# Scan and attention of a hybrid encoder block: one load a chunk, results gathered by the next stage's loads, output product first

## The chip, the cores and the metric

The kernel runs on one core of a Trainium2 chip. The time is device microseconds of one execution, the median of the runs. A core has TensorE (PE in the profile), VectorE (DVE), ScalarE (ACT), GpSimd (POOL) and SyncE (SP), which issues nearly all transfers of this kernel; 16 DMA engines carry them. Each engine works through a queue of its own in order, and so does SyncE: a transfer that waits for something holds up all that are queued behind it.

## What is computed

One layer for 2048 tokens of 1024 features and 16 learned meta tokens, float32. One input projection feeds two mixers side by side, their outputs are joined and projected, and a SwiGLU FFN follows:

```python
u = rmsnorm(h, g_mix[l]);  proj = u @ w_in[l]
na_q, na_k, na_v, dn_q, dn_k, dn_v, dn_z, dn_b, dn_a = jnp.split(proj, pts, axis=-1)
y_na = neighbourhood_attention(na_q, na_k, na_v, na_rel_bias[l], rows)   # 8 heads x 64, windows 8 x 16 of a 32 x 64 grid
y_dn = gated_deltanet(dn_q, dn_k, dn_v, dn_z, dn_b, dn_a, ...)           # 4 heads x 128, both directions, chunked scan
h = h + jnp.concatenate([y_na, y_dn], axis=-1) @ w_out[l]
u = rmsnorm(h, g_ffn[l])
h = h + (jax.nn.silu(u @ w_gate[l]) * (u @ w_up[l])) @ w_down[l]
return rmsnorm(h, g_final)[:, N_META:]
```

The scan goes over chunks of tokens with a state of 128x128 per head and direction. For each chunk:

```python
v_new = u_i - einsum('bhck,bhkv->bhcv', w_i, state)
o_i = einsum('bhck,bhkv->bhcv', q_i, state) + einsum('bhij,bhjv->bhiv', qk_i, v_new)
state = state * cd_i[..., None, None] + einsum('bhck,bhcv->bhkv', k_i, v_new)
```

The two directions are summed, normed and gated with z.

## The kernel before

It runs in three phases. **Phase A** (up to about 885 us) is the input projection, with the convolution, the gates and the chunks' triangular inverses beside it. It leaves its results in DRAM: for each of 16 chunks of 128 tokens and each head, `S.dx` holds four 128x128 blocks (raw queries transposed, keys transposed, keys, values), `S.qe` the queries with each direction's decay (`decays`, L846 to L865, stores them at L864), `S.xq` the inverse and the query-key product.

**Phase B** (885 to 1314 us) interleaves attention and scan by hand, in the loop of `phase_b` at L1325. Attention is 32 slots of 4 steps, a slot being one head and 512 queries. A step is scores (`att_s`, L1119 and L1120, then bias and row maximum on VectorE at L1123, the sign of the maximum on GpSimd at L1125, the exponential on ScalarE at L1126), transposition (`att_t`) and product with the values (`att_o`, L1147 to L1149). The score of a step runs two steps ahead of its product with the values. Query loads (`load_q`, L1055) have one buffer and are issued three steps ahead of `split`, which parts them into a high and a low half (ScalarE L1068, GpSimd L1069). Bias loads (`load`, L1062) have two buffers and leave at the first step of the slot before. Value loads (L1076) run four steps ahead. After every two slots the result tile `ys` goes to DRAM in `S.yo` (L1152), and `att_y` copies it from there, DRAM to DRAM, to its columns of `S.y` (L1165); the copy waits for the store to land.

The scan has 16 steps of 8 pieces (4 heads, 2 directions), one piece beside each attention step. `scan_load` (L1175) fetches the next step's two chunks, one for each direction, in three transfers each: keys and values (L1184, 768 KB), that direction's queries (L1186, 256 KB), and `xq` (L1187, 512 KB). The chunks of scan steps 4 to 7 stay in SBUF for steps 8 to 11, with the other direction's queries loaded into the same place. A piece is `scan_a` (keys times state, L1204, and a VectorE step, L1206), `scan_b` (L1214, then two copies to SBUF on ScalarE) and `scan_c`. The last puts two results in one PSUM tile: the state's update (L1236, read by VectorE at L1241) and then the output (L1244 with the old state, L1245), which ScalarE or VectorE takes out at L1249 or L1251. From scan step 8 on `norm` (L1263) norms two finished chunks and gates them with z (loaded at L1258, multiplied on GpSimd at L1259, then VectorE at L69 to L76 and L1284), and stores them to `S.y` (L1287). In scan steps 12 to 15 phase C's first part is called (`following`): it loads the eight pieces of `w_out` and parts them with ScalarE (L1394) and GpSimd (L1395, 128x1024 at a time), in buffers that the scan's chunks leave.

**Phase C** is the out-projection (1314 to 1517 us) and the FFN. For each of 16 row tiles, in the order 8 to 13, 0 to 7, 14, 15, `load` fetches 128 rows of `S.y` (L1433) and of x (L1435) two tiles ahead, `trans` transposes them (L1420, then L1422 and L1423), `project` multiplies with `w_out` (L1467), and `norm` and `finish` prepare the FFN's operands. The rest is the FFN (L1607 and L1683).

The order within each engine's queue is set by a scheduler from the program's order and its own estimates of times. Loads are tied behind the last value load (`A.last`) with `issue_after`.

Of the kernel before, what the change touches and what calls it, by code (L numbers as in the profile page):

```python
# [16 lines left out]
P = 128  # L17
# [804 lines left out]
def pre_unit(tc, S, Q, hp, half):  # L822
# [23 lines left out]
    def decays(n, kq, rows):  # L846
        a, g = divmod(n, 4)
        h, cg = 2 * hp + a, c0 + g * 2
        E = []
        for e, d in ((0, 0), (1, 1), (2, 1)):  # L850
            ex = Q.g.tile([P, 2, P], F32, name=f"E{e}")
            for c in range(2):
                nc.vector.tensor_scalar(ex[:, c], rows[d][:, c], S.gc[:, d * 4 + h, cg + c:cg + c + 1], 0.0,
                                        op0=ALU.subtract, op1=ALU.max if e == 1 else ALU.min)
            nc.scalar.activation(ex, ex, AF.Exp, scale=-1.0 if e == 1 else 1.0)
            if e != 1:
                s = 1 if e == 0 else -1
                nc.gpsimd.affine_select(out=ex, in_=ex, pattern=[[0, 2], [s, P]], compare_op=ALU.is_ge, fill=0.0,
                                        base=0, channel_multiplier=-s)
            E.append(ex)  # L860
        for d in range(2):
            nc.scalar.activation(rows[d], rows[d], AF.Exp)
            nc.gpsimd.tensor_tensor(rows[d], rows[d], kq[:, :, 0], ALU.mult)
            nc.sync.dma_start(S.qe[d, cg:cg + 2, h].rearrange("c p i -> p c i"), rows[d])  # L864
        return E  # L865
# [161 lines left out]
def attention_loads(tc, S, es, rel):  # L1027
# [36 lines left out]
    def split(n):  # L1064
        s = A.slots[n]
        s.q1 = kp.tile([P, 512], F32R, name="q1")
        s.q2 = kp.tile([P, 512], F32R, name="q2")
        nc.scalar.copy(s.q1, s.qr)  # L1068
        nc.gpsimd.tensor_tensor(s.q2, s.qr, s.q1, ALU.subtract)  # L1069
# [17 lines left out]
def phase_b(tc, S, A, W, norm_g, following):  # L1087
# [4 lines left out]
    with ExitStack() as es:  # L1092
# [46 lines left out]
        def att_o(i):  # L1139
# [10 lines left out]
            if a == 1 and k == 3:  # L1150
                n = i // 8
                nc.sync.dma_start(S.yo[n].rearrange("k r c e -> (r c) k e"), ys[0].rearrange("p k a d -> p k (a d)"))  # L1152
                yq.append((s, S.yo[n]))

        yq = []

        def att_y():

            while yq:
                s, yo = yq.pop()  # L1160
                e0 = s.h // 2 * P
                k = 0
                for C, R0, R1 in s.segs:
                    dst = S.y.rearrange("(g f c) d -> f g c d", f=4, c=16)[C, R0 * 8:R1 * 8, :, e0:e0 + P]
                    nc.sync.dma_start(dst, yo[k:k + R1 - R0].rearrange("k r c e -> (k r) c e"))  # L1165
                    k += R1 - R0
# [7 lines left out]

        def scan_load(s):  # L1175
            cs = (s, 15 - s)
# [5 lines left out]
            for d, c in enumerate(cs):  # L1182
                if c in new:
                    nc.sync.dma_start(dxt[c][:, :, 1:4], S.dx[c, :, :, 1:4].rearrange("h p a i -> p h a i"))  # L1184
                if s != 8:
                    nc.sync.dma_start(dxt[c][:, :, 0], S.qe[d, c].rearrange("h p i -> p h i"))  # L1186
                nc.sync.dma_start(xqt[d, c], S.xq[d, c].rearrange("h p a i -> p h a i"))  # L1187
# [6 lines left out]
        def scan_a(i):  # L1194
            s, h, d, c = geo(i)
            ld = dxt[c][:, h]
# [3 lines left out]
            if S_ is None:  # L1200
                sc[i] = ld[:, 3]
                return
            pa = pz_.tile([P, P], F32, name="z")
            nc.tensor.matmul(pa, ld[:, 1], S_, start=True, stop=True)  # L1204
            R = sp.tile([P, P], F32, name="R", bufs=3)
            nc.vector.scalar_tensor_tensor(R, pa, S.neg_eg[:, dh, col], ld[:, 3], op0=ALU.mult, op1=ALU.add)  # L1206
# [20 lines left out]
        def scan_c(i):  # L1227
# [6 lines left out]
            pc = pz_.tile([P, 2, P], F32, name="z")  # L1234
            if s < 15:
                nc.tensor.matmul(pc[:, 1], dxt[c][:, h, 2], vn[:, 1], start=True, stop=True)  # L1236
# [6 lines left out]
            if S_ is not None:  # L1243
                nc.tensor.matmul(pc[:, 0], dxt[c][:, h, 0], S_, start=True, stop=False)  # L1244
            done[i] = nc.tensor.matmul(pc[:, 0], xqt[d, c][:, h, 1], vn[:, 0], start=S_ is None, stop=True)  # L1245
            if s == 7:
                nc.sync.dma_start(dxt[c][:, h, 0], S.qe[1 - d, c, h])
# [5 lines left out]
        def norm_load(s):  # L1253
            N = Ctx()
            N.z = []
            for c in (s, 15 - s):
                z = sp.tile([P, 4, P], F32, name="z", bufs=2)
                nc.sync.dma_start(z, S.zx[c * P:(c + 1) * P, :].rearrange("p (h d) -> p h d", h=4))  # L1258
                nc.gpsimd.tensor_tensor(z, z, bc(S.ng.rearrange("p (o d) -> p o d", o=1), [P, 4, P]), ALU.mult)  # L1259
# [3 lines left out]
        def norm(s):  # L1263
# [17 lines left out]
            for j, c in enumerate(cs):  # L1281
# [5 lines left out]
                nc.sync.dma_start(S.y[c * P:(c + 1) * P, 512:1024].rearrange("p (h d) -> p h d", h=4), z)  # L1287
# [37 lines left out]
        for i in range(N + 4):  # L1325
# [6 lines left out]
            if i % 4 == 0 and i < 124:  # L1332
                with tc.issue_after(A.last.ins):
                    A.load(i // 4 + 1)
# [10 lines left out]
            if i % 4 == 3:  # L1345
                att_y()
# [28 lines left out]
def phase_c(tc, S, W, wes, x, w_out, g_ffn, w_gate, w_up, w_down, g_final, out):  # L1375
# [11 lines left out]
    with ExitStack() as ps_es:  # L1387
# [3 lines left out]
        def split(hl, src, eng=nc.vector):  # L1391
            raw = st.tile(list(src.shape), F32, name="yu")
            nc.sync.dma_start(raw, src)
            nc.scalar.copy(hl[:, 0], raw)  # L1394
            eng.tensor_tensor(hl[:, 1], raw, hl[:, 0], ALU.subtract)  # L1395
# [3 lines left out]
        for k in range(KB):  # L1399
            wo.append(split(W.tile([P, 2, D], F32R, name="w"), w_out[:, k], nc.gpsimd))  # L1400
# [29 lines left out]
        def load(j):  # L1430
            rows = slice(order[j] * P, (order[j] + 1) * P)
            yt = st.tile([P, D], F32, name="yu")
            nc.sync.dma_start(yt, S.y[rows, :])  # L1433
# [322 lines left out]
def scratch(tc, es):  # L1756
# [7 lines left out]
    S.yo = [dp.tile([4, 8, 16, P], F32, name=f"yo{i}") for i in range(16)]  # L1764
    S.zx = dp.tile([NT, 512], F32, name="zx")
    S.dx = dp.tile([16, 4, P, 4, P], F32, name="dx")
    S.qe = dp.tile([2, 16, 4, P, P], F32, name="qe")
# [4 lines left out]
    S.y = dp.tile([NT, D], F32, name="y")  # L1772
# [132 lines left out]
```

## Time and profile before

| | us |
|---|---|
| median of 3 runs | 2909.57 (2900.05 to 2914.04) |
| the profiled execution | 2900.0 |
| its span, first to last instruction | 2898.0 |
| TensorE busy | 2750.9 (95%) |
| VectorE busy | 1772.8 (61%) |
| ScalarE busy | 1170.8 (40%) |
| GpSimd busy | 754.4 (26%) |

All times below are from the start of the span. In a line of the order of time the engine comes before the source line, and what stands in brackets is how long the engine had been idle and what ended it. "x2" after a group's name means that two instructions were merged into one line, whose time then covers both. The granted clock is a share of TensorE's full 2.4 GHz; its other level is 1.2 GHz, so a mean between 0.5 and 1 tells how long it stood at either.

### The profile page before, as it was taken

The numbers are of one execution on the slowest core, as the hardware profiler recorded it, in microseconds if no ns is written. First come the engines' busy times: TensorE is split into PE (matmuls) and PEld (weight loads), VectorE is DVE, ScalarE is ACT, GpSimd is POOL, SyncE is SP. The second block draws the span as 40 slices with busy tenths as digits, with TensorE's granted clock in tenths as the row PEclk, the third lists the DMA queues.
The fourth block names the chain that finished last, engine by engine and source line by source line (L and its number), as shares of the span: only waits on it lengthen the run. The fifth ranks groups of instructions, "written<-read, shape, count | busy, mean of one in ns | idle before, by whom it ended". The sixth has DMA issues, their size and how long they took to land.

```text
span 2898.0 us, 45796 instructions
## 1 busy us (share of the span) xinstructions
PE 2750.9 (95%) x16364; PEld 2407.7 (83%) x16364; DVE 1772.8 (61%) x3900; ACT 1170.8 (40%) x2733; POOL 754.4 (26%) x769
## 2 busy tenths in 40 slices
PE   8999988988988989879999999999999999999998
PEld 8998988988888988868887888887887888888886
DVE  5897466895643546774667655554547665554354
ACT  4652333652415656752334333333434333233342
POOL 2353353341511112241225223210104322320010
PEclk9999999999999998979999999999999999999999
DMA  4675655566869988985535222236353222225452
GB/s 151 190 203 146 163 156 141 163 179 175 210 159 280 287 231 241 302 258 185 182 126 169 88 80 80 84 116 251 129 183 113 84 88 87 73 95 200 141 177 71
DMA packets 396096, 466.31 MB, mean 161 GB/s; under 512 B 92083, under 2 KB 300300, under 8 KB 394302
## 3 DMA queue, kind: packets, MB, share of 16 engines
q1 hardware_dynamic: 394142, 457.11, 52.0%
q0 software_dynamic: 1728, 6.29, 0.6%
q8 instruction: 129, 2.11, 0.3%
q14 instruction: 97, 0.79, 0.1%
HBM read 334.14 MB, written 141.15 MB: 164 GB/s over the span
## 4 chain that ended last, share of the span: by engine, by line
PE 53%; DVE 3%; DMA 2%; issue 1%; ACT 1%; POOL 0%; SPq 0%; DVEq 0%; ACTq 0%; POOLq 0%
PE pg L1607 24%; PE pg L1683 8%; PE pd L1467 6%; PE pd L1683 4%; PE tp L1683 4%; PE pd L1607 4%; PE y L1147 1%; DVE z L1284 1%; PE tp L1420 0%; DVE w L1451 0%; PE tp L1493 0%; DMA b<-in_rel_dram 0%; DMA k<-kx 0%; POOL s L1555 0%; PE y L1133 0%
## 5 line engine op out<-in xcount | busy, mean ns | idle before, releaser
L405 PE MATMUL acc<-uh,wf 128*128 128x384 f32 (+5 forms) x1920 | 470.0, 329 | 3.0 <-ACT uh L342 1.9
L1451 DVE TENSOR_TENSOR w<-rw,w 128x512 fp32r<-128x512 f32 x308 | 244.0, 794 | 251.2 <-ACT w L1450 250.4
L1607 PE MATMUL pg<-T,w 128*128 128x512 f32 x1584 | 393.9, 397 | 2.6 <-ACT T L1450 1.3
L1607 PE MATMUL pg<-B,w 128*128 128x512 f32 x1584 | 387.9, 397 | 3.5 <-ACT B L1450 2.9
L1450 ACT CAST w<-rw 128x512 fp32r<-128x512 f32 x308 | 190.3, 620 | 485.8 <-PE tp L1683 252.4
L1607 PEld LDWEIGHTS pg<-B,w 128*128 128x128 f32 x1584 | 299.0, 189 | 77.7 <-ACT B L1450 3.3
L1607 PEld LDWEIGHTS pg<-T,w 128*128 128x128 f32 x1584 | 298.2, 188 | 76.0 <-ACT T L1450 1.8
L405 PEld LDWEIGHTS acc<-uh,wf 128*128 128x128 f32 x1920 | 340.2, 192 | 5.7 <-ACT uh L342 2.0
L405 PE MATMUL acc<-ul,wf 128*128 128x384 f32 (+5 forms) x960 | 312.5, 326 | 0.0
L1683 PE MATMUL pg<-w,hT 128*128 128x512 f32 x1056 | 260.9, 395 | 1.9 <-ACT hT L1450 1.8
L1555 POOL TENSOR_TENSOR s<-rw 128x512 f32<-128x512 f32 x88 | 119.5, 1358 | 546.7 <-DMA rw<-in_w_gate_dram 262.4
L1683 PEld LDWEIGHTS pg<-w,hT 128*128 128x128 f32 x1056 | 198.1, 188 | 50.8 <-ACT hT L1450 2.2
L429 PE MATMUL acc<-wn,uh 128*128 128x256 f32 (+3 forms) x1056 | 209.9, 298 | 10.6 <-DVE vs L473 10.3
L1451 DVE TENSOR_TENSOR w<-s,w 128x512 fp32r<-128x512 f32 x176 | 131.6, 750 | 133.9 <-ACT w L1450 132.8
L1450 ACT CAST w<-s 128x512 fp32r<-128x512 f32 x176 | 108.6, 620 | 234.4 <-PE pg L1607 140.4
L405 PEld LDWEIGHTS acc<-ul,wf 128*128 128x128 f32 x960 | 184.8, 192 | 0.8
L429 PEld LDWEIGHTS acc<-wn,uh 128*128 128x128 f32 (+1 forms) x1056 | 172.6, 197 | 13.8 <-DVE vs L473 10.7
L499 DVE SCALAR_TENSOR_TENSOR ct<-cr,cw,ct 128x1024 f32<-128x1024 f32 (+1 forms) x96 | 138.0, 1444 | 37.4 <-ACT ct L497 36.3
L242 POOL TENSOR_TENSOR wf<-raw,wf 128x512 fp32r<-128x512 f32 x80 | 119.6, 1509 | 157.7 <-ACT wf L241 134.5
L1467 PE MATMUL pd<-w,yh 128*128 128x512 f32 x512 | 159.9, 394 | 0.0
L429 PE MATMUL acc<-wn,ul 128*128 128x256 f32 (+3 forms) x528 | 157.4, 298 | 2.4 <-DVE rx_i L58 2.4
L1621 DVE TENSOR_TENSOR eg<-pg,eg 128x512 f32<-128x512 f32 x110 | 76.0, 690 | 106.1 <-PE pg L1607 106.1
(359 smaller groups left out, 5325.8 us busy)
## 6 DMA issues: line engine op xcount, KB each, us to landing
rw<-in_w_down_dram SPq DMA_DIRECT2D x88, 512.0 KB
rw<-in_w_gate_dram SPq DMA_DIRECT2D x44, 512.0 KB
rw<-in_w_up_dram SPq DMA_DIRECT2D x44, 512.0 KB
hd<-eg SPq DMA_DIRECT2D x88, 256.0 KB
s<-hd SPq DMA_DIRECT2D x88, 256.0 KB
raw<-in_w_feat_dram SPq DMA_DIRECT2D x80, 256.0 KB
w<-dx SPq DMA_DIRECT2D x24, 768.0 KB
xq<-xq SPq DMA_DIRECT2D x32, 512.0 KB
```

What stands on the lines that cost most here:

```text
L242: nc.gpsimd.tensor_tensor(lo, raw, hi, ALU.subtract)
L405: nc.tensor.matmul(ps[:, 0:c1 - c0], hl[:, a, k, :], (U.h, U.l)[l][ci][:, k, c0:c1], start=(i == 0), stop=(i == 23))
L429: nc.tensor.matmul(ps[0:np_, 0:n], (U.h, U.l)[l][ci][:, k, off:off + np_], hl[:, a, k, 0:n], start=(i == 0), stop=(i == 23))
L499: nc.vector.scalar_tensor_tensor(tt, raw[:, j:j + T], cw[:, b, j:j + 1], tt, op0=ALU.mult, op1=ALU.add)
L1147: nc.tensor.matmul(po, t.pT[0:w, c], t.v[0:w, c], start=(c == 0), stop=(c == nch - 1))
L1450: nc.scalar.copy(dst_h, src)
L1451: eng.tensor_tensor(dst_l, src, dst_h, ALU.subtract)
L1467: nc.tensor.matmul(ps, (yh, yl)[a][:, k], wo[k][:, b, cs], start=(i == 0), stop=(i == 23))
L1555: nc.gpsimd.tensor_tensor(s, p, q, op)
L1607: nc.tensor.matmul(ps, w[:, a, k], t[:, b, k], start=(k == 0 and (a, b) == (0, 0)), stop=(k == 3 and a == 1))
L1621: nc.vector.tensor_tensor(dst, ps, x0, ALU.add)
L1683: nc.tensor.matmul(acc[j][hf], hk[f][:, a, j * P:(j + 1) * P], wk[f][hf][:, b], start=(f == 0 and i == 0), stop=(f == NFF - 1 and i == 2))
```

## The change

- `S.dx` gets a fifth block a chunk and head. The decayed queries of the forward direction replace the raw ones in block 0, those of the backward direction go to block 4, and `S.qe` is gone. A chunk's first load takes blocks 0 to 3 or 1 to 4 in one transfer of 1 MB; `place` says where queries, keys and values then lie. Only the other direction's queries are still loaded alone.
- In `scan_c` the output's two products come first, then the state's update.
- `S.yo` holds all attention results in one array by head pair, column block and row block. `att_y` is gone, and so are the attention's columns of `S.y`. The out-projection's `load` takes the scan's half of a tile with one transfer and the attention's half with eight, each of 16 partitions and 4 x 512 bytes.
- The bias load of slot n leaves at the last step of slot n - 2 instead of the first step of slot n - 1.
- The subtractions on GpSimd at L1069 and L1259 are done in two halves each. Those at L1395 go to VectorE and, with ScalarE's copies at L1394, are done in halves of 128x512.

```diff
@@ decays
-            nc.sync.dma_start(S.qe[d, cg:cg + 2, h].rearrange("c p i -> p c i"), rows[d])
+            nc.sync.dma_start(S.dx[cg:cg + 2, h, :, 4 * d].rearrange("c p i -> p c i"), rows[d])
@@ split (queries)
-        nc.gpsimd.tensor_tensor(s.q2, s.qr, s.q1, ALU.subtract)
+        for c in (slice(0, 256), slice(256, 512)):
+            nc.gpsimd.tensor_tensor(s.q2[:, c], s.qr[:, c], s.q1[:, c], ALU.subtract)
@@ att_o, att_y
             if a == 1 and k == 3:
-                n = i // 8
-                nc.sync.dma_start(S.yo[n].rearrange("k r c e -> (r c) k e"), ys[0].rearrange("p k a d -> p k (a d)"))
-                yq.append((s, S.yo[n]))
...
-            while yq:
-                s, yo = yq.pop()
-                e0 = s.h // 2 * P
                 k = 0
                 for C, R0, R1 in s.segs:
-                    dst = S.y.rearrange("(g f c) d -> f g c d", f=4, c=16)[C, R0 * 8:R1 * 8, :, e0:e0 + P]
-                    nc.sync.dma_start(dst, yo[k:k + R1 - R0].rearrange("k r c e -> (k r) c e"))
+                    nc.sync.dma_start(S.yo[s.h // 2, C, R0:R1].rearrange("k r c e -> (r c) k e"),
+                                      ys[0][:, k:k + R1 - R0].rearrange("p k a d -> p k (a d)"))
                     k += R1 - R0
@@ scan_load
                 if c in new:
-                    nc.sync.dma_start(dxt[c][:, :, 1:4], S.dx[c, :, :, 1:4].rearrange("h p a i -> p h a i"))
-                if s != 8:
-                    nc.sync.dma_start(dxt[c][:, :, 0], S.qe[d, c].rearrange("h p i -> p h i"))
+                    place[c] = (0, 1, 2, 3) if d == 0 else (3, 0, 1, 2)
+                    nc.sync.dma_start(dxt[c], S.dx[c, :, :, d:d + 4].rearrange("h p a i -> p h a i"))
+                elif s != 8:
+                    nc.sync.dma_start(dxt[c][:, :, place[c][0]], S.dx[c, :, :, 4 * d].rearrange("h p i -> p h i"))
@@ scan_c
+            q, k = (dxt[c][:, h, place[c][n]] for n in (0, 2))
+            if S_ is not None:
+                nc.tensor.matmul(pc[:, 0], q, S_, start=True, stop=False)
+            done[i] = nc.tensor.matmul(pc[:, 0], xqt[d, c][:, h, 1], vn[:, 0], start=S_ is None, stop=True)
             if s < 15:
-                nc.tensor.matmul(pc[:, 1], dxt[c][:, h, 2], vn[:, 1], start=True, stop=True)
+                nc.tensor.matmul(pc[:, 1], k, vn[:, 1], start=True, stop=True)
...
-            if S_ is not None:
-                nc.tensor.matmul(pc[:, 0], dxt[c][:, h, 0], S_, start=True, stop=False)
-            done[i] = nc.tensor.matmul(pc[:, 0], xqt[d, c][:, h, 1], vn[:, 0], start=S_ is None, stop=True)
             if s == 7:
-                nc.sync.dma_start(dxt[c][:, h, 0], S.qe[1 - d, c, h])
+                nc.sync.dma_start(q, S.dx[c, h, :, 4 * (1 - d)])
@@ norm_load, norm
-                nc.gpsimd.tensor_tensor(z, z, bc(S.ng.rearrange("p (o d) -> p o d", o=1), [P, 4, P]), ALU.mult)
+                for h in range(0, 4, 2):
+                    nc.gpsimd.tensor_tensor(z[:, h:h + 2], z[:, h:h + 2], bc(S.ng.rearrange("p (o d) -> p o d", o=1), [P, 2, P]), ALU.mult)
...
-                nc.sync.dma_start(S.y[c * P:(c + 1) * P, 512:1024].rearrange("p (h d) -> p h d", h=4), z)
+                nc.sync.dma_start(S.y[c * P:(c + 1) * P, :].rearrange("p (h d) -> p h d", h=4), z)
@@ the loop of phase_b
-            if i % 4 == 0 and i < 124:
+            if (i == 0 or i % 4 == 3) and i < 120:
                 with tc.issue_after(A.last.ins):
-                    A.load(i // 4 + 1)
+                    A.load((i + 1) // 4 + 1)
...
-            if i % 4 == 3:
-                att_y()
@@ phase_c
-        def split(hl, src, eng=nc.vector):
+        def split(hl, src):
             raw = st.tile(list(src.shape), F32, name="yu")
             nc.sync.dma_start(raw, src)
-            nc.scalar.copy(hl[:, 0], raw)
-            eng.tensor_tensor(hl[:, 1], raw, hl[:, 0], ALU.subtract)
+            for c in (slice(0, 512), slice(512, D)):
+                nc.scalar.copy(hl[:, 0, c], raw[:, c])
+                nc.vector.tensor_tensor(hl[:, 1, c], raw[:, c], hl[:, 0, c], ALU.subtract)
...
-            wo.append(split(W.tile([P, 2, D], F32R, name="w"), w_out[:, k], nc.gpsimd))
+            wo.append(split(W.tile([P, 2, D], F32R, name="w"), w_out[:, k]))
@@ load (out-projection)
-            nc.sync.dma_start(yt, S.y[rows, :])
+            nc.sync.dma_start(yt[:, 512:], S.y[rows, :])
+            for r in range(2):
+                for C in range(4):
+                    p = r * 64 + C * 16
+                    R, rr = divmod(order[j] * 2 + r, 8)
+                    nc.sync.dma_start(yt[p:p + 16, 0:512].rearrange("c (h e) -> c h e", h=4),
+                                      S.yo[:, C, R, rr].rearrange("h c e -> c h e"))
@@ scratch
-    S.yo = [dp.tile([4, 8, 16, P], F32, name=f"yo{i}") for i in range(16)]
-    S.dx = dp.tile([16, 4, P, 4, P], F32, name="dx")
-    S.qe = dp.tile([2, 16, 4, P, P], F32, name="qe")
+    S.dx = dp.tile([16, 4, P, 5, P], F32, name="dx")
-    S.y = dp.tile([NT, D], F32, name="y")
+    S.y = dp.tile([NT, 512], F32, name="y")
+    S.yo = dp.tile([4, 4, 4, 8, 16, P], F32, name="yo")
```

## Rows read from the trace of the kernel before

**Rows 1.** Stretches of the span: busy us (instructions) of PE, PEld, DVE, ACT, POOL; clock, DMA share, GB/s

```profile
885.00:1228.00 343.00, 307.29 (x2365) 296.97 (x2366) 199.77 (x805) 219.57 (x718) 68.31 (x141) 0.94 0.93 271
...
1228.00:1314.00 86.00, 66.87 (x440) 62.83 (x439) 65.55 (x214) 49.87 (x146) 35.12 (x41) 0.80 0.83 265
...
1314.00:1517.00 203.00, 203.00 (x1014) 168.62 (x1012) 117.28 (x247) 59.10 (x109) 38.48 (x29) 1.00 0.48 156
```

**Rows 2.** Order of time on TensorE, its longest gaps, 885 to 1270

```profile
982.99 0.49 PE L1214 MATMUL z<-R,xq 128*128 128x128 f32 x2 [4.46 <-ACT oacc L1249]
...
1021.22 0.80 PE L1244 MATMUL z<-S,w 128*128 128x128 f32 x2 [3.25 <-DVE S L1241]
...
1087.80 0.80 PE L1204 MATMUL z<-S,w 128*128 128x128 f32 x2 [3.89 <-ACT oacc L1249]
...
1197.11 0.79 PE L1244 MATMUL z<-S,w 128*128 128x128 f32 x2 [4.41 <-DVE S L1241]
...
1238.91 0.79 PE L1204 MATMUL z<-S,w 128*128 128x128 f32 x2 [6.38 <-DVE R L1206]
...
1266.09 0.79 PE L1244 MATMUL z<-S,w 128*128 128x128 f32 x2 [4.83 <-DVE R L1206]
```

**Rows 3.** Order of time on ScalarE and VectorE, where two of these gaps begin

```profile
981.24 0.62 ACT L1068 CAST q<-qr 128x512 fp32r<-128x512 f32 x1 [5.00 <-DMA qr<-qx]
...
1020.34 0.56 DVE L1123 CUSTOM_DVE_ANT_0 sb<-y,b 128x384 f32<-128x384 f32 x1 [5.00 <-DMA b<-in_rel_dram]
```

**Rows 4.** Order of time on GpSimd and VectorE, 1259 to 1282

```profile
1259.87 4.66 POOL L1395 TENSOR_TENSOR w<-yu,w 128x1024 fp32r<-128x1024 f32 x2 [6.01 <-PE z L1204]
...
1260.19 2.08 DVE L75 TENSOR_SCALAR or_t<-or_t 128x8 f32<-128x8 f32 x1
...
1275.01 1.13 DVE L1284 SCALAR_TENSOR_TENSOR z<-oacc,of,z 128x128 f32<-128x128 f32 x4
...
1276.13 5.36 DVE L1284 SCALAR_TENSOR_TENSOR z<-oacc,of,z 128x128 f32<-128x128 f32 x4
```

**Rows 5.** Waits from 880 to 1320 (SyncE 1330): who for whom, us total, times, longest

```profile
SPq L1165 <- DMA yo<-ys: 24.8, 11, 4.1
...
DVE sb L1123 <- DMA b<-in_rel_dram: 17.0, 7, 5.0
...
PE z L1244 <- DVE S L1241: 11.9, 8, 4.4
```

**Rows 6.** Order of time of SyncE's issues

```profile
963.97 0.38 SPq L1152 DMA_DIRECT2D yo<-ys  x1
...
969.45 0.56 SPq L1165 DMA_DIRECT2D y<-yo  x1
...
972.42 1.09 SPq L1055 DMA_DIRECT2D qr<-qx  x2
...
1195.61 1.69 SPq L1055 DMA_DIRECT2D qr<-qx  x2
```

**Rows 7.** Transfers from 885 to 1314: queue (packets, MB, share), issues (KB each)

```profile
q1 hardware_dynamic: 97607, 115.27, 90.7%
...
y<-yo SPq DMA_DIRECT2D x12, 256.0 KB
...
y<-yo SPq DMA_DIRECT2D x6, 128.0 KB
```

**Rows 8.** Line L1451: count, ns min/median/max, first and last start

```profile
L1451 DVE TENSOR_TENSOR w<-s,w x176: 676/692/1777, 1519.6 to 2619.9; 128x512 fp32r<-128x512 f32 x176
```

**Rows 9.** Order of time, out-projection: a tile's load on SyncE, its transposition on TensorE

```profile
1345.33 0.33 SPq L1433 DMA_DIRECT2D yu<-y  x1
...
1356.31 0.60 PE L1420 MATMUL tp<-ident,yu 128*128 128x128 f32 x4
...
1360.16 0.58 SPq L1433 DMA_DIRECT2D yu<-y  x1
...
1369.02 0.60 PE L1420 MATMUL tp<-ident,yu 128*128 128x128 f32 x4
```

More of the change, by code (lines that the diff above doesn't have):

```diff
@@ L1150, in att_o @@
             if a == 1 and k == 3:
-                n = i // 8
-                nc.sync.dma_start(S.yo[n].rearrange("k r c e -> (r c) k e"), ys[0].rearrange("p k a d -> p k (a d)"))
-                yq.append((s, S.yo[n]))
-        yq = []
-        def att_y():
-            while yq:
-                s, yo = yq.pop()
-                e0 = s.h // 2 * P
                 k = 0
                 for C, R0, R1 in s.segs:
-                    dst = S.y.rearrange("(g f c) d -> f g c d", f=4, c=16)[C, R0 * 8:R1 * 8, :, e0:e0 + P]
-                    nc.sync.dma_start(dst, yo[k:k + R1 - R0].rearrange("k r c e -> (k r) c e"))
+                    nc.sync.dma_start(S.yo[s.h // 2, C, R0:R1].rearrange("k r c e -> (r c) k e"),
+                                      ys[0][:, k:k + R1 - R0].rearrange("p k a d -> p k (a d)"))
                     k += R1 - R0
@@ L1173, in phase_b @@
         dxt, xqt, sc = {}, {}, {}
+        place = {}
         def scan_load(s):
@@ L1195, in scan_a @@
             s, h, d, c = geo(i)
-            ld = dxt[c][:, h]
+            kT, v = (dxt[c][:, h, place[c][n]] for n in (1, 3))
             col = slice(c, c + 1)
@@ L1200, in scan_a @@
             if S_ is None:
-                sc[i] = ld[:, 3]
+                sc[i] = v
                 return
             pa = pz_.tile([P, P], F32, name="z")
-            nc.tensor.matmul(pa, ld[:, 1], S_, start=True, stop=True)
+            nc.tensor.matmul(pa, kT, S_, start=True, stop=True)
             R = sp.tile([P, P], F32, name="R", bufs=3)
-            nc.vector.scalar_tensor_tensor(R, pa, S.neg_eg[:, dh, col], ld[:, 3], op0=ALU.mult, op1=ALU.add)
+            nc.vector.scalar_tensor_tensor(R, pa, S.neg_eg[:, dh, col], v, op0=ALU.mult, op1=ALU.add)
             sc[i] = R
```

## The prediction

> **What bounds the kernel now.** I read the page's slices first (TensorE is nearly full everywhere, least so around the attention and scan), then the busy time by stretch. Three stretches matter [rows 1]: attention beside scan (885 to 1228 us), the scan's end with its norms and the attention that is left (1228 to 1314), and the out-projection (1314 to 1517). In the third TensorE is busy for all 203.0 us at a granted clock of 1.00: nothing can be won there, only lost. In the first it is idle for 343 - 307.3 = 35.7 us, and its clock of 0.94 stretches the busy part by about 307.3 x 0.06 = 18 us. In the second it is idle for 86 - 66.9 = 19.1 us, and the clock of 0.80 costs about 66.9 x 0.2 = 13 us. So 86 of the 2898 us can be touched at all. The transfers are no free resource: the DMA share is 0.93 in the first stretch and 0.83 in the second.
>
> The order of time on TensorE says where the idle time lies [rows 2]. In the first stretch four gaps of 3.25 to 4.46 us make 16.0 of the 35.7 us. TensorE waits for ScalarE or VectorE there, but those had been waiting themselves [rows 3]: ScalarE 5.00 us for a query load at 981.24, VectorE 5.00 us for the bias at 1020.34; the other two gaps look the same. These are late loads. In the second stretch the two longest gaps, 6.38 and 4.83 us, end on VectorE, which was not waiting but slow: at 1260.19 an operation on 128x8 elements took 2.08 us while GpSimd ran two subtractions of L1395 in 4.66 us, and at 1276.13 four multiplies of L1284 took 5.36 us where the four before took 1.13 [rows 4].
>
> **The change, part by part.** All sums are against the profiled execution: a span of 2898.0 in a run of 2900.0 us. The median of the runs shown is 2909.57, 9.6 above it.
>
> *Results gathered by the out-projection.* The 20 copies from yo to y go, and with them their waits: SyncE stood 24.8 us for L1165, 11 times [rows 5]. Behind it in its queue stand the bias, the queries and the values. In front of the gap at 983 a store to yo is issued at 963.97, the copy leaves at 969.45, the queries at 972.42 [rows 6] and land at 981.2: without the wait (24.8/11 = 2.3 us) and the copy's 0.56 us they leave nearly 3 us sooner. In DMA time the queue was busy for 90.7% of 429 us = 389 us [rows 7]; the copies that fall in it are 12 x 256 + 6 x 128 KB = 3.9 of its 115.27 MB, or 7680 of its 97607 packets of 512 B. That is 13 us by bytes and 31 by packets; I take the byte end, the smaller gain.
>
> *One load a chunk.* By the code 24 of the 30 query loads of the scan (256 KB in pieces of 512 bytes, so 512 packets) join their chunk's load: 12288 packets fewer and no byte. Its worth lies between 0 and 12288/97607 x 389 = 49 us of DMA time; I take 0 by the same choice. A first load of 1 MB instead of 768 KB delays the scan's first matmul by about 1 us (256 KB at the 271 GB/s of [rows 1]). The stores to the strided slot in the input projection are as many and as long; TensorE doesn't wait for them, so 0, at most a few us if their landing held the next loads.
>
> *Bias one step earlier.* 32 bias loads leave one step of 429/128 = 3.35 us sooner. The waits of 5.00 us shrink to about 1.7. The new place can wait for VectorE to have read the buffer's last user, on SyncE, with value and key loads behind it; the value loads wait there for a TensorE step of the same age anyhow, so I cost it at nothing, at most a step (3.35 us) where they don't cover it.
> For the four gaps together I take 10 of 16.0 us: 6 of the 7.7 us that end on the bias, 4 of the 8.3 us on queries. A us of idle time brought 18/35.7 = 0.5 us of slow clock in this stretch: 5 us more.
>
> *Output first.* TensorE waited 11.9 us at L1244 for VectorE's state update, 8 times [rows 5]: the two products share a PSUM tile, and the second was started after the first had been read. Two of the eight are gaps on the bias counted above (3.25 and 4.41), so 4.2 us are left; I take 3. The state comes later by two products, but is wanted eight scan steps on: 0.
>
> *Subtractions from GpSimd to VectorE, and in halves.* Eight subtractions of w_out go from GpSimd; six lie in the second stretch. VectorE gets 16 of 128x512, 0.69 us each by the same form in the FFN [rows 8]: 11 us, 12 of them (8.3 us) in the second stretch, where VectorE has 65.6 busy in 86 us, a good part of it the stretched operations. The remaining GpSimd operations in halves hold VectorE up for about half as long. I take 60% of the 19.1 us idle, 11 us, with 13/19.1 = 0.7 us of clock for each, 8 us; and half of the 8.3 us of new VectorE work on the path, -4. The bounds are 0 (new work takes the place of what it held up) and 32 (all idle and slow time).
> The Trainium skill, page "SBUF — State Buffer", section "Who interferes with whom", has a rule for this: a VectorE instruction with two SBUF inputs and a GpSimd instruction that reads SBUF exclude each other, and whoever is first keeps the other out for a whole instruction. The rows agree. By it the new subtraction, with two SBUF inputs, is itself held up by what stays on GpSimd, which speaks for the -4.
>
> *The out-projection's loads.* Each of 16 row tiles now takes 9 loads for y instead of one: 128 more issues. Two issues together took 1.09 us [rows 6], so a tile's nine take about 5 us. A landing took 969.45 - 963.97 - 0.38 = 5.1 us in the full queue: an upper bound, since the DMA share is 0.48 here [rows 1]. The time at hand is 11.0 us for one tile (1345.33 to 1356.31) and 8.9 for the next (1360.16 to 1369.02) [rows 9], and so on in turn. 10.1 us would be 1.2 too late on every second tile, 8 us in all; at half the landing nothing is late. I take 1 and keep 0 to 8.
>
> Sum: 10 + 5 + 3 - 1 = 17 in the first stretch, 11 + 8 - 4 = 15 in the second, -1 in the third: 31 us. What is late next limits it. If the two first stretches need 389 - 13 = 376 us of DMA time at the same share of 0.907, they last 415 us, 14 less than 429. I take 25, between the two. 2900.0 - 25 = 2875, and as the median lay 9.6 above this run, **2885**.
>
> **Rivals.** *The waits only move.* Queries still queue behind 1 MB loads, VectorE's new work fills what it no longer loses, and only the products' order and some of SyncE's waits pay: 3 + 3, **2903**. For it: the DMA share near 1, and that a bias load put earlier stands no longer behind the queries but ahead of other loads. Against: 24.8 us of waiting on SyncE really goes.
> *All late loads and all held-up operations go.* If packets count and not bytes (31 + 49 us of DMA time), both stretches lose most of their idle and slow time: 55 of 86 us, **2855**.
> *The gather is late: slower than before.* An issue can cost more: two took 1.69 us at 1195.61 [rows 6]. Nine at 0.85 with a landing of 5.1 us are 12.7 us, 3.8 over 8.9 and 1.7 over 11.0, on 14 tiles 38 us; less the 25 won that is +13, **2923**. It decides from a load of about 11.8 us on, where lateness eats the gain; TensorE would then show a gap before every transposition of a tile.
> The Trainium skill, "DMA: Bandwidth & Descriptors", section "Bandwidth", has the rule behind this rival: batch transfers to 1 MiB, for under 64 KB the descriptors dominate; the eight pieces have 32 KB each. No row here shows transfers of 32 KB one after another.
> *It doesn't do what it says*: if a tile's gather had to wait for the last store, which by the code follows the last attention step, the first tile's load would land one store and one load after the second stretch ends: two times 5.1 us, with TensorE idle once for about 10. 2885 + 10 = 2895 stays within the forecast's own range.
>
> **How the numbers follow.** Forecast 2885 (2870 to 2897): 0.45. Waits only move, 2903: 0.28. All go, 2855: 0.14. Late gather, 2923: 0.13. The range reaches to 2855 below and 2917 above, leaving out the lower half of the third case and most of the last. About 0.5% (14.5 us, so below 2895 or above 2924, and for the last case nearly at its edge) is what a measurement of this kernel can tell from no change: faster 0.56 (most of the forecast and all of the third case), same 0.32, slower 0.12.
>
> **What would show it.** After: no L1165; L1123 waiting for the bias a few us in total instead of 17.0 [rows 5]; L1244 never behind L1241; 128x8 operations of VectorE under 0.5 us throughout; the clock of the second stretch above 0.9; L1467 without gaps. Wrong: gaps before L1420, ScalarE still 5 us behind query loads, or VectorE over 80% busy from 1228 us on with TensorE waiting for it.

## The result, and the profile after

The changed kernel takes 2887.46 us (median of 20 runs, 2875.16 to 2899.24); the kernel before, on the same chip, 2906.25 us (20 runs, 2894.99 to 2914.04). The ratio is 0.9935, with a 95% interval of 0.9922 to 0.9948: some 19 us less (15 to 23). The profiled execution has a span of 2881.9 us.

The stretches of [rows 1] in the changed kernel (length; busy us and instructions of PE, PEld, DVE, ACT, POOL; granted clock, DMA share, GB/s):

```profile
885.00:1228.00 343.00, 310.68 (x2442) 303.11 (x2441) 204.13 (x837) 229.11 (x753) 73.76 (x178) 0.93 0.92 271
1228.00:1314.00 86.00, 71.28 (x438) 64.70 (x438) 52.49 (x207) 42.92 (x123) 19.48 (x40) 0.84 0.73 239
1314.00:1517.00 203.00, 202.01 (x1001) 166.97 (x1000) 123.28 (x254) 62.71 (x115) 50.36 (x37) 1.00 0.50 159
```

TensorE is 3.4 us busier in the first stretch and 4.4 us in the second, and the second stretch's clock is 0.84 instead of 0.80. That is less than was hoped for at either place, and the third stretch is about as full as before (202.0 of 203 us). Since the kernel is further on at a given time, the same stretches hold a little different work. So a mark in the program is better: the first transposition of a finished row tile (`tp<-ident,rt`), which stands early in the out-projection. In the profiled execution of every kernel here the span ends 1546 to 1551 us after it, so what a kernel wins shows in its start. It is 1350.8 us before, and in the changed kernel (count, duration in ns, first and last start):

```profile
L1495 PE MATMUL tp<-ident,rt x64: 270/272/273, 1335.2 to 1511.1; 128*128 128x128 f32 x64
```

15.6 us earlier, of a span that is 16.1 us shorter: all of the gain lies ahead of this mark.

The waits that answer to [rows 5], 880 to 1320 us (who for whom: us in total, times, longest). The bias, the copies (L1165) and the wait of the output's product for the state are gone from the list. The wait for queries has grown:

```profile
ACT q L1068 <- DMA qr<-qx: 51.1, 12, 8.7
```

In the kernel before, ScalarE waited for queries 35.4 us, 16 times, 5.2 at the longest. TensorE's gaps of the first stretch [rows 2] are no fewer and no shorter, and three of the long ones, with the longest of the second stretch, now stand behind a query load (order of time on TensorE, then on ScalarE; in brackets how long the engine had been idle, and what ended it).

```profile
983.36 0.80 PE L1232 MATMUL z<-S,w 128*128 128x128 f32 x2 [4.26 <-ACT vn L1217]
...
1026.55 0.80 PE L1199 MATMUL z<-S,w 128*128 128x128 f32 x2 [5.13 <-ACT oacc L1245]
...
1083.50 0.89 PE L1134 MATMUL y<-ident,sb 128*104 128x128 f32 x3 [3.84 <-ACT sb L1127]
...
1281.50 0.91 PE L1134 MATMUL y<-ident,sb 128*128 128x128 f32 x3 [6.19 <-ACT sb L1127]
```

```profile
982.27 0.62 ACT L1068 CAST q<-qr 128x512 fp32r<-128x512 f32 x1 [4.44 <-DMA qr<-qx]
...
1025.71 0.62 ACT L1068 CAST q<-qr 128x512 fp32r<-128x512 f32 x1 [7.38 <-DMA qr<-qx]
...
1082.28 0.62 ACT L1068 CAST q<-qr 128x512 fp32r<-128x512 f32 x1 [5.67 <-DMA qr<-qx]
...
1280.22 0.62 ACT L1068 CAST q<-qr 128x512 fp32r<-128x512 f32 x1 [7.67 <-DMA qr<-qx]
```

The last of them is new in kind: the gaps of 6.38 and 4.83 us behind a slow VectorE [rows 2] are gone, and one of 6.19 us has come, at the end of attention. The order of SyncE's issues (start, us) shows why this query load is late:

```profile
1261.49 1.23 SPq L1055 DMA_DIRECT2D qr<-qx  x2
...
1265.23 1.80 SPq L1434 DMA_DIRECT2D yu<-yo  x3
...
1269.92 0.43 SPq L1429 DMA_DIRECT2D yu<-y  x1
...
1270.87 1.37 SPq L1434 DMA_DIRECT2D yu<-yo  x3
...
1273.18 3.26 SPq L1434 DMA_DIRECT2D yu<-yo  x5
1276.55 1.24 SPq L1055 DMA_DIRECT2D qr<-qx  x2
```

Between two query loads stand 14 gather issues (L1434) of the out-projection's first row tiles, 0.36 to 0.65 us each. Attention is not done yet. Six of the 14 belong to the first row tile and eight to the second, by their order behind each tile's load of `S.y` (L1429). TensorE transposes the first tile while attention is still running, so that one is wanted soon, but the second only well after the last query load (order of time on TensorE):

```profile
1272.10 1.91 PE L1416 MATMUL tp<-ident,yu 128*128 128x128 f32 x8
...
1295.37 0.60 PE L1416 MATMUL tp<-ident,yu 128*128 128x128 f32 x4
```

### The profile page after: what moved, and what is told of

It is laid out like the page before. It is cut to its first block, busy times and chain, and to the rows that moved or that the text cites. A ratio compares the mean times of both kernels' runs of the same rounds, so it can differ in the third digit from the quotient of the medians.

```text
span 2881.9 us, 45992 instructions
## 1 busy us (share of the span) xinstructions
PE 2740.7 (95%) x16364; PEld 2400.2 (83%) x16364; DVE 1758.0 (61%) x3916; ACT 1170.4 (41%) x2741; POOL 744.4 (26%) x809
## 4 chain that ended last, share of the span: by engine, by line
PE 54%; DMA 3%; DVE 2%; ACT 0%; issue 0%; POOL 0%; SPq 0%; DVEq 0%; ACTq 0%; POOLq 0%
PE pg L1609 24%; PE pg L1685 8%; PE pd L1469 6%; PE pd L1685 4%; PE tp L1685 4%; PE pd L1609 4%; DMA rt<-ut 1%; DMA z<-zx 1%; PE y L1148 1%; DMA k<-kx 0%; PE tp L1495 0%; PE tp L1416 0%; DMA qr<-qx 0%; DVE w L1453 0%; PE y L1134 0%
```

## The experiments

Five kernels make one part of the change alone, on the kernel before; five take one part back out of the changed kernel; two alter the changed kernel's order on SyncE. All in one table: ratio to the kernel before with its 95% interval, that in us (of 2902, the middle of the medians of the kernel before), and the mark of the profiled execution. By their intervals, two ratios must lie some 0.002 to 0.0035 (6 to 10 us) apart to be told apart; the mark comes from one execution and is no better than a few us.

| kernel | ratio | us | mark, us |
|---|---|---|---|
| before | 1 | 0 | 1350.8 |
| changed | 0.9935 (0.9922 to 0.9948) | -18.9 | 1335.2 |
| p_pool: VectorE/halves alone | 0.9943 (0.9922 to 0.9964) | -16.5 | 1339.5 |
| p_gather: gather alone | 0.9985 (0.9970 to 0.9999) | -4.4 | 1342.0 |
| p_bias: bias earlier alone | 0.9989 (0.9979 to 1.0000) | -3.2 | 1349.3 |
| p_order: output first alone | 0.9973 (0.9959 to 0.9988) | -7.8 | 1342.2 |
| p_merge: one load a chunk alone | 0.9979 (0.9962 to 0.9995) | -6.1 | 1343.9 |
| u_pool: changed, but GpSimd as before | 0.9954 (0.9934 to 0.9975) | -13.3 | 1341.3 |
| u_gather: changed, but copies as before | 0.9931 (0.9906 to 0.9956) | -20.0 | 1335.3 |
| u_bias: changed, but bias as before | 0.9908 (0.9888 to 0.9928) | -26.7 | 1327.4 |
| u_order: changed, but state first | 0.9917 (0.9891 to 0.9944) | -24.1 | 1331.3 |
| u_merge: changed, but two loads a chunk | 0.9945 (0.9925 to 0.9965) | -16.0 | 1341.7 |
| fix_tail: changed, out-projection's first loads behind the last queries | 0.9892 (0.9872 to 0.9913) | -31.3 | 1328.7 |
| fix_ub: fix_tail and u_bias | 0.9894 (0.9869 to 0.9918) | -30.8 | 1325.1 |

**Subtractions to VectorE, in halves: alone and taken back.** The edit of p_pool on the kernel before (u_pool is the same, undone in the changed kernel):

```diff
-        nc.gpsimd.tensor_tensor(s.q2, s.qr, s.q1, ALU.subtract)
+        for c in (slice(0, 256), slice(256, 512)):
+            nc.gpsimd.tensor_tensor(s.q2[:, c], s.qr[:, c], s.q1[:, c], ALU.subtract)
...
-            eng.tensor_tensor(hl[:, 1], raw, hl[:, 0], ALU.subtract)
+            for c in (slice(0, 512), slice(512, D)):
+                nc.scalar.copy(hl[:, 0, c], raw[:, c])
+                nc.vector.tensor_tensor(hl[:, 1, c], raw[:, c], hl[:, 0, c], ALU.subtract)
```

> The kernel before with one part of the change: the subtractions of w_out go to VectorE in halves, those of the query split and the products of z stay on GpSimd in halves. Theory (held-up VectorE): the gain lies in the scan's end, 15 us by the prediction's own term (11 idle, 8 clock, less 4 of new work), so about 2891; VectorE's four multiplies of L1284 take 1.1 to 1.3 us for one each time they come up instead of 5.36 at 1276.13 in the kernel before, and the stretch from 1228 us on has a clock above 0.80. Rival (new work takes the place of what it held up): within 4 us of the kernel before.

> The changed kernel with the subtractions back on GpSimd and in one piece, the rest stands. Theory (the held-up VectorE is a cost of its own in the scan's end): 13 to 16 us slower than the changed kernel, 0.9985 of the kernel before, with VectorE operations on 128x8 of over 1 us again beside long GpSimd operations. Rival (with the output first and the loads freed the scan's end no longer waits for VectorE): within 5 us of the changed kernel.

Alone it gave 16.5 us, where 15 were forecast, and at the forecast place. The second stretch of p_pool (columns as above):

```profile
1228.00:1314.00 86.00, 73.74 (x484) 67.39 (x483) 60.61 (x228) 50.78 (x152) 24.68 (x47) 0.90 0.89 282
```

TensorE is busy for 73.7 instead of 66.9 us, at 0.90 instead of 0.80; the first stretch (308.05 us busy, clock 0.94) is as in [rows 1]. What has gone with it are the long hold-ups of [rows 4]. In the second stretch (VectorE's groups: busy us in total, mean ns of one), before, in u_pool and in p_pool:

```profile
L75 DVE TENSOR_SCALAR or_t<-or_t 128x8 f32<-128x8 f32 x9 | 4.3, 483 | 0.1
```

```profile
L75 DVE TENSOR_SCALAR or_t<-or_t 128x8 f32<-128x8 f32 x9 | 4.5, 498 | 0.2
```

```profile
L75 DVE TENSOR_SCALAR or_t<-or_t 128x8 f32<-128x8 f32 x9 | 1.5, 166 | 0.1
```

Two long ones make the mean in u_pool (2.23 and 1.07 us); its median is 0.17. The longest multiply of z in this stretch takes 2465 ns before, 2459 in u_pool and 850 ns in p_pool, where the median is 340 in all three: the hold-ups are shorter, not all gone. The new VectorE work did not fill the place: the rival falls. But taken back out of the changed kernel the part is worth only 5 us (0.9954 beside 0.9935, the mark 6.1 us later), at the edge of what can be told, short of the 13 to 16 expected and near the 5 of its rival, though the long operations are back. Why they cost so little there, no run shows.

**Output first: alone and taken back.**

```diff
             pc = pz_.tile([P, 2, P], F32, name="z")
+            if S_ is not None:
+                nc.tensor.matmul(pc[:, 0], dxt[c][:, h, 0], S_, start=True, stop=False)
+            done[i] = nc.tensor.matmul(pc[:, 0], xqt[d, c][:, h, 1], vn[:, 0], start=S_ is None, stop=True)
             if s < 15:
                 nc.tensor.matmul(pc[:, 1], dxt[c][:, h, 2], vn[:, 1], start=True, stop=True)
...
-            if S_ is not None:
-                nc.tensor.matmul(pc[:, 0], dxt[c][:, h, 0], S_, start=True, stop=False)
-            done[i] = nc.tensor.matmul(pc[:, 0], xqt[d, c][:, h, 1], vn[:, 0], start=S_ is None, stop=True)
```

> The kernel before with one part alone: in the last piece of a scan step the output's products come before the state's. Prediction's term: TensorE no longer waits at the output's product for VectorE's state update (11.9 us, 8 times, of which 4.2 were not counted elsewhere), 3 us faster, about 2903. Rival (another wait takes its place at once): the wait is gone from the list and the time within 1 us. Rival (what the wait held up was more than its own length, as the clock falls after idle time): 6 us or more.

> The changed kernel with the state's product first again. The order alone gave 8.9 us where the prediction's term was 3. Theory (its waits are partly those that the other parts shorten too): 3 us slower than the changed kernel, 0.9945 of the kernel before, with the waits of TensorE at the output's product for VectorE's state update back in the list. Rival (a gain of its own): 8 us or more slower, 0.996 and above.

Alone it gave 7.8 us, more than twice the 3 of the sum, and in the changed kernel nothing (if anything it costs). The wait says why it has nothing left there. It was 11.9 us, 8 times, in the kernel before [rows 5]; with the state first, it is in p_pool, in p_gather, in p_merge and in p_bias (one line each, in that order):

```profile
PE z L1245 <- DVE S L1242: 10.8, 7, 3.5
```

```profile
PE z L1233 <- DVE S L1230: 6.9, 6, 3.3
```

```profile
PE z L1250 <- DVE S L1247: 6.2, 6, 4.0
```

```profile
PE z L1244 <- DVE S L1241: 3.7, 4, 1.6
```

and in u_order, with all four other parts:

```profile
PE z L1240 <- DVE S L1237: 1.3, 2, 0.7
```

The subtractions alone hardly shorten it, the gather, the one load and the bias each by 5 to 8 us, and all four nearly end it: much of it was other lateness, passed on by VectorE. Once that is gone the order has nothing left to remove. (Each edit also makes the scheduler place the instructions anew, so these kernels differ by more than their edit; how many us come from that, no run here shows.)

**Bias one step earlier: alone and taken back.**

```diff
-            if i % 4 == 0 and i < 124:
+            if (i == 0 or i % 4 == 3) and i < 120:
                 with tc.issue_after(A.last.ins):
-                    A.load(i // 4 + 1)
+                    A.load((i + 1) // 4 + 1)
```

> The kernel before with one part alone: each bias load leaves one step earlier. Prediction's term: 6 us of waits and 3 of clock, so 9 us faster, about 2897, and the waits of VectorE for the bias fall from 17.0 us to a few. Rival (the waits move to the queries): the bias waits go, but ScalarE waits as much longer for the query loads, which now stand behind the bias in the queue: within 3 us of the kernel before.

> The changed kernel with the bias loads put back one step later. Theory (bias waits only move to the query loads): VectorE waits again for the bias, ScalarE less for the queries (51.1 us in the changed kernel), and the time stays within 4 us of the changed kernel. Rival (prediction's term): 9 us slower than the changed kernel. Rival (the earlier bias load delays the queries and costs more than it brings once the copies are gone): faster by 4 us or more.

Alone it gave 3.2 us (0 to 6 by the interval), not the 9 of the sum. In p_bias the wait for the bias falls from 17.0 us to 1.5, and the wait for the queries rises from 35.4 to 45.3 us:

```profile
ACT q L1068 <- DMA qr<-qx: 45.3, 17, 7.0
...
DVE sb L1123 <- DMA b<-in_rel_dram: 1.5, 1, 1.5
```

In u_bias, with the bias late again and all else of the change:

```profile
ACT q L1068 <- DMA qr<-qx: 39.5, 15, 4.8
DVE sb L1124 <- DMA b<-in_rel_dram: 7.7, 4, 3.3
```

Both waits together: 52.4 us before, 46.8 with the bias alone, 51.1 in the changed kernel, 47.2 without this part. The wait moves from one load to the other. The totals are no price by themselves: in u_pool both waits come to 35.5 us, and it is no faster than the changed kernel. But in the company of the other parts moving the bias seems to cost more than it brings: u_bias is 8 us faster than the changed kernel by the ratios (intervals overlap by a little) and 7.8 by the mark, and the first stretch's clock is 0.97 instead of 0.93. A late bias holds its engine up by 3.3 us at the longest there, a late query load in the changed kernel by 8.7. What makes the queries later is argued only. In the changed kernel the bias loads wait on SyncE for VectorE (by the code, until it is done with what the buffer held before),

```profile
SPq L1062 <- DVE R L1201: 10.0, 10, 2.9
```

where in u_bias no entry of theirs for VectorE is above 1.1 us in total; and a bias load's bytes also stand ahead of others' in the queue. A third bias buffer, with which the load could leave early without that wait, would tell the two apart; it was not tried.

**Gather: alone, taken back, and its first issues put last.** p_gather and u_gather add or undo the parts of the diff at `yo`, `att_y`, `S.y` and the out-projection's `load`. fix_tail is the changed kernel with:

```diff
-            nc.sync.dma_start(s.qr[d * 64:(d + 1) * 64].rearrange("p (f n) -> p f n", f=len(s.segs)),
+            A.lq = nc.sync.dma_start(s.qr[d * 64:(d + 1) * 64].rearrange("p (f n) -> p f n", f=len(s.segs)),
...
                 es2.close()
-                following()
+                with tc.issue_after(A.lq.ins):
+                    following()
```

> The kernel before with one part alone: the copies from yo to y and their waits on SyncE go, and the out-projection's loads gather the results in eight pieces. Prediction's term: 4 us of late query loads, 2 of clock, 1 lost in the out-projection, so 5 us faster, about 2901. Theory (the gather costs in attention's tail): the issues of the first two or three tiles, nine each, stand on SyncE ahead of the last query load, ScalarE waits for that load for over 5 us where the kernel before has no such wait near the end, and the sum is within 3 us of the kernel before. Rival (bytes and packets of the copies bind): 13 to 31 us faster, about 2875 to 2893. Rival (the loads are late): TensorE shows gaps ahead of the transpositions of the out-projection, and it is slower by over 5 us.

> The changed kernel with the copies from yo to y back and one load a row tile in the out-projection. Alone the gather gave 4.6 us. Theory (its gain in attention's first part is spent on the nine issues a tile ahead of the last query load, 12 us by the run that moved them): faster than the changed kernel by 3 to 8 us, about 0.991, no wait over 4 us of ScalarE for a query load from 1270 us on, SyncE waiting for the copies again by some 20 us. Rival (the freed queue is worth more than the tail loses): 5 us slower, about 0.995.

> The changed kernel with one thing added: the out-projection's first issues are placed behind the last query load in SyncE's queue. Theory (the gather's first issues delay attention's tail): the wait of 7.67 us of ScalarE at 1280 goes or falls below 3 us, the gap of 6.19 us on TensorE with it, and as a us of idle time takes up to one of slow clock there, 5 to 9 us faster than the changed kernel. Rival (something else is late next in the tail, such as the norms of the last chunks): the wait goes, and the time stays within 3 us.

Besides the gather, this edit puts the other first loads of the out-projection behind the queries, those of x and of the FFN's norm weights, 512 KB each.

Alone, the gather gave 4.4 us (5 forecast), without a late query load near the end: there the scan ended late enough that only six gather issues and one of y came between the last two query loads. In the changed kernel the scan ends earlier, the out-projection's first loads are released earlier, and 14 come in between. With them put behind the queries, the last two loads arrive so (fix_tail, order of time on ScalarE; the stretch beneath):

```profile
1264.37 0.62 ACT L1068 CAST q<-qr 128x512 fp32r<-128x512 f32 x1 [0.87 <-DMA qr<-qx]
...
1273.85 0.62 ACT L1068 CAST q<-qr 128x512 fp32r<-128x512 f32 x1 [2.83 <-DMA qr<-qx]
```

```profile
1228.00:1314.00 86.00, 75.01 (x473) 68.27 (x472) 56.72 (x217) 43.56 (x126) 20.62 (x42) 0.92 0.77 246
```

7.67 us of waiting became 2.83, the gap of 6.19 us on TensorE one of 2.31, and in the stretch TensorE is busy 3.7 us longer, at 0.92 instead of 0.84. The kernel takes 2874.47 us, ratio 0.9892: 12 us faster than the changed kernel with intervals that don't meet (5 to 9 were expected), 6.5 by the mark. With the copies back, in u_gather, the loads of x and of the norm weights still stand ahead of the last two query loads, and ScalarE waits for no query load from 1228 us on: what makes the last one late in the changed kernel are the gather's issues, not those loads. Their number alone does not set the wait, though. Between the last two query loads stand 14 of them in the changed kernel (7.67 us of waiting), 12 in u_merge (3.43) and in u_bias, 7 in u_order (1.49), 6 in p_gather and 4 in u_pool (none), and in u_bias the last query load costs only this:

```profile
1270.68 0.62 ACT L1068 CAST q<-qr 128x512 fp32r<-128x512 f32 x1 [2.27 <-DMA qr<-qx]
```

So the gather was worth nothing in the changed kernel (u_gather 0.9931, neither the 3 to 8 us faster of its theory nor the 5 us slower of its rival), which fits a gain ahead that is spent in the tail. fix_tail is 11 us faster than u_gather (0.9931 - 0.9892, intervals that overlap by little). That is not the gather's worth alone, as fix_tail moved the other loads too; u_gather with those loads moved would tell, and was not run.

**One load a chunk: alone and taken back.** The edit is the part of the diff at `scan_load`, `place` and `S.dx`; p_merge keeps the products' old order.

> The kernel before with the one load a chunk alone, the products in their old order. Prediction's term: 1 us slower (the first load is 256 KB longer), the packets saved worth nothing, so about 2905 beside 2903. The four other parts alone gave 16.0, 4.6, 3.3 and 8.9 us by their medians, 32 or so together, and the whole change gave 18.8. Theory (this part costs): some 10 us slower, because a chunk's longer load stands in SyncE's queue ahead of query, bias and value loads that are wanted at once. Rival (packets count): up to 49 us faster; any gain over 10 us speaks for it. Rival (the parts overlap, this one is neutral): within 4 us.

> The changed kernel with the one load a chunk taken back: queries again have a tensor and loads of their own, the four other parts stand. Theory (the one load costs): faster than the changed kernel by some 10 us, about 2875. Rival (the parts overlap): within 4 us of the changed kernel, 0.9935 of the kernel before. Rival (the one load is what frees the DMA queue for the others): slower than the changed kernel by 5 us or more, with waits of ScalarE and VectorE for loads above those of the changed kernel.

Alone 6.1 us faster, taken back 3 us slower (not told apart; the mark says 6.5): the theory that this part costs falls, and it is a small gain. Its price in DMA time can be read by itself. Queue q1 from 885 to 1300 us (packets, MB, share) in the changed kernel, then in u_merge:

```profile
q1 hardware_dynamic: 79005, 111.70, 89.2%
```

```profile
q1 hardware_dynamic: 91521, 111.00, 90.8%
```

In 415 us that is 370.2 against 376.8 us: 12516 packets fewer (the prediction counted 12288) and 0.7 MB more for 6.6 us less. By the queue's mean (370.2/111.70 = 3.3 us a MB) 0.7 MB are 2.3 us, so the packets saved are worth about 9 us of DMA time by this estimate, between the 0 taken and the 49 of the other end. The kernel before (94888 packets, 111.24 MB, 90.8%) and p_merge (84282, 113.77, 90.4%) give about 10 us by the same reckoning.

**Both remedies at once.**

> The changed kernel with two things altered at once: the bias loads at their old place (alone 7.8 us faster than the changed kernel, by the ratios 0.9908 and 0.9935 to the kernel before) and the out-projection's first issues behind the last query load (alone 12.4 us faster, 0.9892). Theory (two separate places, first stretch and tail): the gains add, about 0.9865, 2863 beside 2902. Rival (both work on the same wait for query loads): about 0.989, no better than the better of the two.

They don't add: 2873.03 us, ratio 0.9894, as fix_tail alone, though the mark is 3.6 us earlier. The 0.9865 of a full sum lies just outside the interval. In u_bias the tail's query load was waited for only 2.27 us, so fix_tail's part had little left to remove there. Either is faster than the kernel before and than the changed kernel; fix_tail is the smaller edit.

## Why the prediction was right

2885 was forecast and 2887.5 came, well inside 2855 to 2917, and faster by over 0.5% as thought likeliest. That the two lie 2.5 us apart is in part luck. The forecast took 25 us off 2909.57, the median of three runs; over 20 runs the kernel before has 2906.25, and the gain is 18.9 us, three quarters of what was forecast. The parts of the sum erred in both directions, and point by point it was right for reasons that only half held.

- *Subtractions* (15): right in place, mechanism and size when alone (16.5), its clock nearly (0.90; "above 0.9" was asked of the whole change). In company it is worth only 5. The Trainium skill's rule of the exclusion between VectorE and GpSimd (page "SBUF — State Buffer", section "Who interferes with whom") agrees: with GpSimd's long operations gone L75 is back from 0.50 to 0.17 us. That operation has a single input, so it is the section's clause on `tensor_scalar`, which can take the shared ports too, that fits it; the one on two inputs that the prediction quoted fits the multiplies of L1284, from 2465 ns at the longest to 850.
- *Output first* (3): alone 7.8, in company nothing. The term took away the two gaps that it knew to be the bias's; it didn't see that the other six of the eight waits were in good part passed-on lateness as well (1.3 us of 11.9 are left in u_order). Why alone it gave more than its term is open: ScalarE and VectorE wait for queries and bias as long as before (38.6 and 21.0 us).
- *Bias* (6, and 3 of clock): this step failed. "The waits of 5.00 us shrink to about 1.7" held for the bias, and the queries took over the wait. The step compared the load with its old place only; it named what stands behind the load on SyncE and then "cost it at nothing", because value loads wait there anyhow. The query loads, not the values, were next to be late. That was the first rival's mechanism ("the waits only move"), true for this part and not for the rest.
- *Gather* (4 of the query gaps, 2 of clock, -1 in the out-projection): the gain came when alone (4.4). The loss was put in the wrong place. In the out-projection the nine loads a tile cost nothing: TensorE is busy for 202.0 of 203 us, so the rival of a late gather is out. But the first tiles' issues are made while attention still runs, and of the queues that a moved step passes, SyncE's at that point was not looked at: up to 12 us (fix_tail, which moved other first loads as well).
- *One load a chunk* (-1): the delay of the first loads is 3.5 us and not 1 (TensorE's first wait for `xq`: 3.57 us in the changed kernel and in u_pool, 3.54 in p_merge, none in the kernel before and in u_merge), but the packets were worth some 9 us of DMA time, and the part as a whole gains 3 to 6.
- *The limit* (31 cut to 25): a cut was needed, but its reason was not what the runs show. The five parts alone add up to 38 us (give or take 10 by their intervals), the whole gives 18.9. Parts that shorten the same wait (that for the state, above) are one reason. The larger one found is a cost that the parts bring on only together: the late query load in the tail. With that mended, and the other first loads moved with it, the whole gives 31.3 (fix_tail). By DMA time, 14 us were estimated; over the same 429 us (885 to 1314) the queue's busy time fell from 389 to 374.5 us, near the 376 of the estimate; but the estimate held the share fixed at 0.907, and it fell to 0.873.

Of what was to show it, four came as asked: no L1165, no bias wait, no wait of the output's product for the state, no gaps in the out-projection. A fifth nearly came: VectorE's operations on 128x8 take 0.69 us at the longest (2.26 before; under 0.5 was asked). Two did not: the clock of the second stretch is 0.84 where above 0.9 was asked, and ScalarE is more than 5 us behind query loads, which the prediction had named as a sign that it was wrong. It was, there; that the terms that were too low when alone (order, packets) and those that were too high (bias, tail) came out near the forecast is luck.

## What to carry to other kernels

Parts that shorten waits didn't add up here, where the waits hang on one queue: look for the load that is late next, and take the sum of the parts for an upper end. When a transfer is split into many or moved, look at each place where its issues enter the queue, above all the first ones, which may stand ahead of the last loads of the stage before; tying that stage's first loads behind those was worth 12 us here, beside the 19 of the whole change. A load that leaves earlier stands ahead of something: name it before counting the gain.

## What the hardware showed that had not been expected

- The number of packets counts, but far less than in proportion: 12516 packets fewer (14%) took 6.6 us (1.8%) off the queue's busy time, or about 9 us with the 0.7 MB set off, an estimate by the queue's mean time for a MB.
- Issues of 32 KB pieces cost SyncE 0.36 to 0.65 us each (the 14 above), and that and their place ahead of the last query load, not their landing, was their price here. The Trainium skill ("DMA: Bandwidth & Descriptors", section "Bandwidth") calls transfers under 64 KB descriptor-dominated, by loads issued from GpSimd; issued from SyncE, eight such pieces a tile left the out-projection's TensorE without a gap.
- The granted clock of a stretch doesn't simply follow TensorE's busy time in it. In the 86 us from 1228 on it was 0.92 with 75.0 us busy (fix_tail), 0.90 with 73.7 (p_pool) and 0.84 with 71.3 (changed kernel), but 0.80 with 74.3 (u_bias), 0.82 with 74.7 (u_merge) and 0.88 with 79.5 (fix_ub). Part of that is in the measure: at a lower clock the same instructions are busy for longer (402 matmul records in the 74.3 us of u_bias, 473 in the 75.0 of fix_tail). The prediction's 0.7 us of clock for a us of idle time is near the first three (0.55, 0.60 and 0.77) and far from the last three (1.2 to 1.5); what else sets the clock, these runs don't show.
